# An encoder layer on one core: a fifth pair of weight row blocks by seven products, its low parts by an adding transfer

## The chip, the cores and the metric

The kernel runs on one core of a Trainium2 chip. The metric is the device time of one execution in microseconds (us), the median of several. The engines are named as in the profile: PE (TensorE matmul, PEld its weight load), DVE (VectorE), ACT (ScalarE), POOL (GpSimd), SP (SyncE, which issues most transfers). Each engine works through its own list of instructions in order and waits at an instruction until what it needs is there.

## The reference

One layer of a bidirectional encoder, 256 tokens of width 2048, all in float32:

```python
x = x + 0.5 * swiglu(rms_norm(x, ffn1_norm), ffn1_w_gu, ffn1_w_down)   # gate, up: 2048 -> 5632 each
proj = rms_norm(x, mix_norm) @ w_in            # query, key, value of two groups of heads
x = x + concat(group_A, group_B) @ w_out       # grouped-query and differential attention
x = x + 0.5 * swiglu(rms_norm(x, ffn2_norm), ffn2_w_gu, ffn2_w_down)
x = rms_norm(x, out_norm)

def swiglu(h, w_gu, w_down):
    g, u = split(h @ w_gu, 2)
    return (silu(g) * u) @ w_down
```

## The kernel before

Every float32 weight and activation is split in two parts, hi (a cast by ACT, L139) and lo (the weight minus hi, by DVE, L140), and every product is three matmuls: hi·hi, hi·lo, lo·hi. Weights come from HBM into `raw` (4 slots; two row blocks of 128 rows, j = 0 and 1, 1024 columns). ACT writes `whi`, DVE writes `wlo`; both have 4 slots, so two `raw` tiles are split ahead of PE, and slots are taken in turn: a row block takes the slot that the fourth row block before it had.

The two feed-forward parts (FFN) are the same code. The first 1024 gate columns and then the first 1024 up columns are done by `mm_block`. The other gate and up columns are done 512 at a time in `columns(i)`, i = 2 to 10; one call takes the 16 row blocks of the contraction in 8 pairs, for 512 gate columns (s = 0) and the same 512 up columns (s = 1). After each call but the last of an FFN comes one `down`, half of a group of the down projection (96 matmuls). So there are 18 calls of `columns` in all.

`PAIRS` says how a pair is done. False: 8 products (2 row blocks, 2 token halves, gate and up), 24 matmuls. True: 7 products after Strassen and Winograd, 21 matmuls. They need sums of weight blocks, which DVE forms in `Ta` and `Tb` (1024 columns each, L443, L445, L446) and which are split like weights (`Ta_hi`, `Ta_lo`, `Tb_hi`, `Tb_lo`, one slot each); of the second row block only the gate half is still split. The sums of x that the products need (`xs` for False, `xp` for True) are formed once in each FFN from `xT`, by functions put in the list `pending`, of which `pump()` runs one at set places.

`turn_block` brings 512 finished columns of gate times up into the layout of the next product: a transposition on DVE, 16 transfers of 32 KB on SP (`move`, L282), then two casts and two subtractions into `hT_hi` and `hT_lo`. `down` needs these.

The text of the program doesn't set the order on the engines: a scheduler sorts the instructions of each engine, before the run, by its own estimate of when each can start, and that order is then fixed. With c for the pair, the weights are split thus:

```python
n = 1 if pair and j == 1 else 2
splits.append(split(hi[:, :n], lo[:, :n], raw[:, j, :n]))
```

Of the kernel before, what the change touches and what calls it, by code (L numbers as in the profile page):

```python
# [20 lines left out]
P = 128  # L21
# [17 lines left out]
PAIRS = (False, True, False, True, False, True, False, True)  # L39
# [4 lines left out]
def encoder_layer(ctx: ExitStack, tc: tile.TileContext, a: dict, out: bass.AP):  # L44
# [96 lines left out]

    def new_rows():

        return (ht_p.tile([P, WB // P, T], F32R, name="hT_hi"), ht_p.tile([P, WB // P, T], F32R, name="hT_lo"))
# [31 lines left out]
    def mm_block(lhs, nk, w, row0, col0, width, evac, before=None, after=None, slots=1, t_major=None):  # L176
# [39 lines left out]
        if t_major is not None:  # L216
            with tc.manual_schedule(engines={mybir.EngineType.PE}):
                for c in range(nc_):
                    load(c)
                    for b in range(nb):  # L220
                        mm(b, 0, [2 * c, 2 * c + 1])
                        if c == nc_ - 1:
                            evac(b, 0, ps[b, 0])
                for b in range(nb):
                    step = 256 if b == nb - 1 else 512
                    for c0 in range(0, 512, step):
                        mm(b, 1, list(range(nk)), c0, c0 + step)
                        evac(b, 1, ps[b, 1], c0, c0 + step)
            return
        for c in range(nc_):  # L230
            if before is not None:
                before(c)
            load(c)
# [20 lines left out]
    def ffn(xT, norm, w_gu, w_down, half_done=None, before=None, after=None, last_evac=None, last_pools=None):  # L254
# [4 lines left out]
        with tc.tile_pool(name="ffn", bufs=1) as fp:  # L259
# [40 lines left out]
            sg = [fp.tile([P, WB], F32, name=f"sg{t}") for t in range(NT)]  # L300

            def evac_gate(b, t, ps):
                nc.scalar.activation(sg[t][:, b * 512:(b + 1) * 512], ps, AF.Silu, scale=norm.rstd[t][:, 0:1])

            if before is None:
                mm_block(rows(xT), NK, w_gu, 0, 0, WB, evac_gate)
            else:
                with tc.manual_schedule(engines={mybir.EngineType.SP}):
                    mm_block(rows(xT), NK, w_gu, 0, 0, WB, evac_gate, lambda c: before(c, ip), after)
            h0 = [fp.tile([P, NT, 512], F32, name="h", bufs=2) for b in range(2)]  # L310

            def evac_up(b, t, ps):
                nc.vector.scalar_tensor_tensor(h0[b][:, t, :], ps, norm.rstd[t][:, 0:1],
                                               sg[t][:, b * 512:(b + 1) * 512], op0=ALU.mult, op1=ALU.mult)


# [4 lines left out]
            rb = fp.tile([P, T], F32, name="rb")  # L321
# [26 lines left out]
            def paired_rows(c):  # L348
# [12 lines left out]
            pending.append(spread)  # L361
            pending.extend(functools.partial(paired_rows if pair else single_rows, c)
                           for c, pair in enumerate(PAIRS))
            ready = []
            pending.append(lambda: ready.append(True))
# [3 lines left out]
            for b in range(2):  # L369
                turn_block(b, h0[b])  # L370


            def columns(i):
# [9 lines left out]
                def mm(name, terms, end):  # L383
# [31 lines left out]
                for c, pair in enumerate(PAIRS):  # L415
# [5 lines left out]
                    for j in range(2):  # L421
# [3 lines left out]
                        splits.append(split(hi[:, :n], lo[:, :n], raw[:, j, :n]))  # L425
# [31 lines left out]
                    if c == last:  # L457
                        while pending:
# [5 lines left out]
                             ("p1", "p6", "p7", "c12", "c11", "c3", "c21"))  # L464
                    for m, name in enumerate(names):
                        mm(name, [product[name]], c == last)
                        if c == last:
                            done(name)
                        if m in (2, 6):
                            pump()  # L470
                turn_block(i, h)

            def down(j, half):
                c, width = j * WB, min(WB, DFF - j * WB)
                final = j == n_groups - 1
                while not set(range(2 * j, 2 * j + width // 512)) <= turned_blocks:
                    pump()
# [5 lines left out]
                mm_block(rows([hT[j]]), width // P, w_down, c, half * WB, WB, evac, slots=2, t_major=t_major)  # L483
# [16 lines left out]
    def load_xT(c, pool):  # L500

        raw = pool.tile([P, 2, 512], F32, name=("Ta", "Tb")[c % 2]).rearrange("p j f -> p (j f)")[:, :2 * T]
# [31 lines left out]
    with ExitStack() as mixer:  # L534
        mp = mixer.enter_context(tc.tile_pool(name="mix", bufs=1))
# [248 lines left out]
        def new_oT():  # L784
            return (mp.tile([P, WB // P, T], F32R, name="oT_hi", bufs=2),
                    mp.tile([P, WB // P, T], F32R, name="oT_lo", bufs=2))
# [117 lines left out]
```

## Time and profile before

| | |
|---|---|
| time, median of 3 | 1756.95 us (1756.93 to 1759.1) |
| the profiled execution, its own time | 1757.13 us |
| its span, first to last instruction | 1755.4 us |
| PE busy | 1731.7 us, 99% |
| DVE busy | 1400.5 us, 80% |
| ACT busy | 958.3 us, 55% |
| POOL busy | 48.2 us, 3% |
| bytes moved by the DMA engines | 355.81 MB |

The time of the profiled execution is 0.2 us over the median. Between its own time and its span lie 1.7 us at the two ends. A PE that reads as busy is not a PE at its peak, since matmuls overlap; what counts is how far apart they start.

### The profile page before, as it was taken

How to read it: one execution, taken by the hardware profiler on the slowest of the kernel's cores; microseconds unless marked ns; L12 is line 12 of the kernel's file. 1: busy time of each engine (PE TensorE's matmuls, PEld its weight loads, DVE VectorE, ACT ScalarE, POOL GpSimd, SP SyncE). 2: the span in 40 equal slices, each digit the busy share in tenths (PEclk: the TensorE clock that was granted, in tenths of full speed). 3: DMA queues.
4: the chain of work that ended last, by engine and by line, in shares of the span. 5: the costliest groups of instructions: out<-in, count | busy, mean ns of one | idle time of the engine just before them, and what ended most of it. 6: DMA issues, size and time to landing. Idle time of an engine off the chain costs nothing.

```text
span 1755.4 us, 21389 instructions
## 1 busy us (share of the span) xinstructions
PE 1731.7 (99%) x7652; PEld 1423.7 (81%) x7652; DVE 1400.5 (80%) x1729; ACT 958.3 (55%) x1359; POOL 48.2 (3%) x75
## 2 busy tenths in 40 slices
PE   9998999999999999999999999999999999999998
PEld 7876888888888888888788888867888888888886
DVE  6988989889889887646566565998889888988976
ACT  6555555555455554656776455555455455555544
POOL 0000000000000000122110000000000000000000
PEclk9999999999999999999999999999999999999999
DMA  9546665576566664655445455565566557656662
GB/s 368 189 161 216 212 237 193 176 248 210 183 245 204 203 209 162 219 189 196 156 173 195 145 199 184 173 232 189 202 214 220 185 201 242 205 186 240 220 227 98
DMA packets 165259, 355.81 MB, mean 203 GB/s; under 512 B 15600, under 2 KB 42656, under 8 KB 165024
## 3 DMA queue, kind: packets, MB, share of 16 engines
q1 hardware_dynamic: 164336, 353.10, 58.4%
q8 instruction: 60, 0.98, 0.2%
q10 hardware_dynamic: 720, 1.31, 0.2%
q14 instruction: 47, 0.39, 0.1%
q0 software_dynamic: 96, 0.02, 0.0%
HBM read 337.60 MB, written 2.10 MB: 194 GB/s over the span
## 4 chain that ended last, share of the span: by engine, by line
PE 90%; DMA 3%; DVE 2%; ACT 2%; SPq 2%; issue 1%; POOL 0%; POOLq 0%; ACTq 0%; DVEq 0%
PE psm L213 16%; PE psm L214 16%; PE psm L212 16%; PE psm L386 12%; PE psm L388 12%; PE psm L389 12%; DMA raw<-in_ffn_w_gu 1%; DMA raw<-in_w_in 1%; DVE wlo L140 1%; PE psx L386 1%; SPq L632 1%; PE psx L389 1%; PE psx L388 1%; DMA raw<-in_ffn_w_down 1%; SPq L282 1%
## 5 line engine op out<-in xcount | busy, mean ns | idle before, releaser
L140 DVE TENSOR_TENSOR wlo<-raw,whi 128x1024 fp32r<-128x1024 f32 (+1 forms) x644 | 713.7, 1140 | 208.3 <-ACT whi L139 204.2
L139 ACT CAST whi<-raw 128x1024 fp32r<-128x1024 f32 (+1 forms) x644 | 611.5, 984 | 480.3 <-PE psm L389 213.9
L213 PE MATMUL psm<-wlo,hT_hi 128*128 128x512 f32 x1252 | 487.8, 391 | 1.7 <-DVE wlo L140 1.7
L214 PE MATMUL psm<-whi,hT_lo 128*128 128x512 f32 x1252 | 486.3, 390 | 0.0
L212 PE MATMUL psm<-whi,hT_hi 128*128 128x512 f32 x1252 | 428.6, 391 | 4.8 <-ACT whi L139 2.1
L212 PEld LDWEIGHTS psm<-whi,hT_hi 128*128 128x128 f32 x1252 | 235.3, 188 | 56.2 <-ACT whi L139 2.9
L213 PEld LDWEIGHTS psm<-wlo,hT_hi 128*128 128x128 f32 x1252 | 235.8, 188 | 52.2 <-DVE wlo L140 3.6
L214 PEld LDWEIGHTS psm<-whi,hT_lo 128*128 128x128 f32 x1252 | 235.5, 188 | 48.2
L388 PE MATMUL psm<-wlo,xs 128*128 128x512 f32 x576 | 221.5, 390 | 0.7 <-DVE wlo L140 0.7
L389 PE MATMUL psm<-whi,xs 128*128 128x512 f32 x576 | 221.2, 389 | 0.0
L386 PE MATMUL psm<-whi,xs 128*128 128x512 f32 x576 | 196.6, 389 | 0.7 <-ACT whi L139 0.7
L388 PEld LDWEIGHTS psm<-wlo,xs 128*128 128x128 f32 x576 | 108.1, 188 | 24.2 <-DVE wlo L140 1.9
L386 PEld LDWEIGHTS psm<-whi,xs 128*128 128x128 f32 x576 | 108.0, 188 | 23.6 <-ACT whi L139 1.1
L389 PEld LDWEIGHTS psm<-whi,xs 128*128 128x128 f32 x576 | 108.1, 188 | 22.4
L139 ACT CAST Ta_hi<-Ta 128x1024 fp32r<-128x1024 f32 x72 | 75.6, 1051 | 91.0 <-DVE Ta L443 71.3
L443 DVE TENSOR_TENSOR Ta<-raw 128x1024 f32<-128x1024 f32 x72 | 87.9, 1220 | 39.2 <-DMA raw<-in_ffn_w_gu 39.0
L140 DVE TENSOR_TENSOR Tb_lo<-Tb,Tb_hi 128x1024 fp32r<-128x1024 f32 x72 | 87.8, 1219 | 2.7 <-ACT Tb_hi L139 0.8
L249 DVE SCALAR_TENSOR_TENSOR x<-psm,x 128x512 f32<-128x512 f32 (+1 forms) x113 | 73.1, 680 | 19.6 <-PE psm L214 19.4
L140 DVE TENSOR_TENSOR Ta_lo<-Ta,Ta_hi 128x1024 fp32r<-128x1024 f32 x72 | 87.7, 1219 | 0.2 <-ACT Ta_hi L139 0.2
L388 PE MATMUL psm<-wlo,xp 128*128 128x512 f32 x216 | 84.6, 392 | 0.0
L389 PE MATMUL psm<-whi,xp 128*128 128x512 f32 x216 | 84.5, 391 | 0.0
L386 PE MATMUL psm<-whi,xp 128*128 128x512 f32 x216 | 80.5, 390 | 0.4 <-ACT whi L139 0.4
(166 smaller groups left out, 1729.6 us busy)
## 6 DMA issues: line engine op xcount, KB each, us to landing
raw<-in_ffn_w_gu SPq DMA_DIRECT2D x288, 512.0 KB, 5.6
raw<-in_ffn_w_down SPq DMA_DIRECT2D x88, 1024.0 KB, 5.6
raw<-in_w_in SPq DMA_DIRECT2D x32, 1024.0 KB, 5.1
raw<-in_ffn_w_gu SPq DMA_DIRECT2D x30, 1024.0 KB, 5.9
raw<-in_w_out SPq DMA_DIRECT2D x16, 1024.0 KB, 5.0
h<-sg SPq DMA_DIRECT2D x352, 32.0 KB, 1.9
raw<-in_w_in SPq DMA_DIRECT2D x8, 512.0 KB, 3.6
heads<-near SPq DMA_DIRECT2D x96, 32.0 KB, 1.9
```

The costliest lines, as they stand in the source:

```text
L139: casts.append(nc.scalar.copy(hi, src))
L140: return nc.vector.tensor_tensor(lo, src, f32(hi), op=ALU.subtract)
L212: nc.tensor.matmul(o, xh, wh, start=k == 0, stop=False)
L213: nc.tensor.matmul(o, xh, wl, start=False, stop=False)
L214: nc.tensor.matmul(o, xl, wh, start=False, stop=k == nk - 1)
L249: nc.vector.scalar_tensor_tensor(x[t][:, s], ps[:, c0:c1], scale, x[t][:, s], op0=ALU.mult, op1=ALU.add)
L282: nc.sync.dma_start(turned[q * B32:(q + 1) * B32, :, i_, :], near[0][i_ * B32:(i_ + 1) * B32, :, q, :])
L386: nc.tensor.matmul(bank[name], xh, wh, start=name not in begun, stop=False)
L388: nc.tensor.matmul(bank[name], xh, wl, start=False, stop=False)
L389: nc.tensor.matmul(bank[name], xl, wh, start=False, stop=end and m == n - 1)
L443: nc.vector.tensor_tensor(ta, flat[:, 3:4, :].broadcast_to([P, 2, 512]), flat[:, 1:3, :], op=ALU.subtract)
L632: nc.sync.dma_start(far[q * B32:(q + 1) * B32, i], near[i * B32:(i + 1) * B32, q].rearrange("p h d -> p (h d)"))
```

## The change

It has four parts. (1) `PAIRS[0]` becomes True: 5 of 8 pairs by 7 products. (2) For the True pairs 0, 1, 3 and 5 of each call, the lo part of row block j = 0 is no longer a subtraction on DVE. ACT writes minus hi into `wlo`, and then a transfer issued by POOL adds `raw` to it (512 KB, in place). The two matmuls that read this lo part (hi·lo of the products c11 and c3) are written down last in the pair. (3) The sums of x are put in `pending` sooner: after chunk 6 of the first `mm_block` of FFN 1, before the first one of FFN 2. (4) Block 1 of `turn_block` follows block 0 after six idle places, and `down` waits for the block that its chunk reads and not for both. Beside these: `xT` is loaded into three other tiles, `rb` lies in `junk`, and `oT_hi` and `oT_lo` get a pool of their own.

```diff
-PAIRS = (False, True, False, True, False, True, False, True)
+PAIRS = (True, True, False, True, False, True, False, True)
...
+    def split_by_transfer(hi, lo, src):
+        casts.append(nc.scalar.copy(hi, src))
+        nc.scalar.activation(lo, f32(hi), AF.Copy, scale=-1.0)
+        nc.gpsimd.dma_start(f32(lo), src, accum_op=ALU.add)
...
         for c in range(nc_):
             if before is not None:
                 before(c)
+            if need is not None:
+                need(c)
             load(c)
...
+            def after_load(c):
+                after(c)
+                if c == 6:
+                    form_sums()
...
+            if before is None:
+                form_sums()
...
-            for b in range(2):
-                turn_block(b, h0[b])
+            turn_block(0, h0[0])
+            pending.extend([idle] * 6)
+            turn_block(1, h0[1])
...
-                        nc.tensor.matmul(bank[name], xh, wl, start=False, stop=False)
+                        if later is None:
+                            nc.tensor.matmul(bank[name], xh, wl, start=False, stop=False)
+                        else:
+                            later.append((bank[name], xh, wl))
...
-                        splits.append(split(hi[:, :n], lo[:, :n], raw[:, j, :n]))
+                        if pair and j == 0 and c < last:
+                            split_by_transfer(*(part.rearrange("p s f -> p (s f)") for part in (hi, lo, raw[:, j])))
+                        else:
+                            splits.append(split(hi[:, :n], lo[:, :n], raw[:, j, :n]))
...
+                    for o, xh, wl in later:
+                        nc.tensor.matmul(o, xh, wl, start=False, stop=False)
...
-                while not set(range(2 * j, 2 * j + width // 512)) <= turned_blocks:
-                    pump()
+                def need(c):
+                    while 2 * j + c // 2 not in turned_blocks:
+                        pump()
```

How the instructions stand now, at two places. The number behind a tile is that of its buffer, L404, L407, L410 and L497 are matmuls of a pair in the changed program, L219 and L220 matmuls of `down`.

**Start of a call of columns, ACT.** These are rows of ACT where `columns(9)` of FFN 1 begins, before the change: pair 0 is the two casts from `raw_4501`, pair 1 those from `raw_4536`.

```order
L139 CAST whi_4459<-raw_4453 128x1024
L139 CAST Tb_hi_4556<-Tb_4548 128x1024
L139 CAST whi_4504<-raw_4501 128x1024
L139 CAST whi_4508<-raw_4501 128x1024
L139 CAST hT_hi_4449<-h_3989 128x8x2x32 x2
L139 CAST whi_4539<-raw_4536 128x1024
L139 CAST whi_4543<-raw_4536 128x512
L139 CAST Ta_hi_4632<-Ta_4627 128x1024
```

And the same place in the changed program: pair 0 is `raw_4601`, pair 1 `raw_4647`; `whi_4559` is the last row block of the `down` before.

```order
L139 CAST whi_4559<-raw_4553 128x1024
L144 CAST whi_4604<-raw_4601 128x1024
L145 ACTIVATE wlo_4605<-whi_4604 128x1024
L139 CAST whi_4609<-raw_4601 128x512
L144 CAST whi_4650<-raw_4647 128x1024
L139 CAST whi_4655<-raw_4647 128x512
L145 ACTIVATE wlo_4651<-whi_4650 128x1024
L139 CAST hT_hi_4549<-h_4075 128x8x2x32 x2
L139 CAST Ta_hi_4664<-Ta_4659 128x1024
```

The write of minus hi for pair 1 (`wlo_4651`) now stands behind the cast into `whi_4655`, and the casts of `hT_hi` and `Ta_hi_4664` behind it. `whi_4655` takes the slot of `whi_4559`, four row blocks before.

**Start of a call of columns, PE.** First the end of `down` in PE's list of the changed program, with the last matmul that reads `whi_4559`:

```order
L219 MATMUL psm_4458<-wlo_4560,hT_hi_3501 128x512
L220 MATMUL psm_4458<-whi_4559,hT_lo_3502 128x512
L497 MATMUL psm_4594<-wlo_4605,xp0_129 128x512
L497 MATMUL psm_4595<-wlo_4605,xp0_129 128x512
L404 MATMUL psm_4594<-whi_4650,xp0_129 128x512
L410 MATMUL psm_4594<-whi_4650,xp1_130 128x512
```

From the row behind that L220 on, 21 matmuls stand ahead of the first that reads `wlo_4651`, the tile that the transfer of pair 1 completes:

```order
L407 MATMUL psm_4597<-wlo_4656,xp0_129 128x512
L410 MATMUL psm_4597<-whi_4655,xp1_130 128x512
L404 MATMUL psm_4596<-Tb_hi_4622,xp0_129 128x512
L407 MATMUL psm_4596<-Tb_lo_4623,xp0_129 128x512
L410 MATMUL psm_4596<-Tb_hi_4622,xp1_130 128x512
L497 MATMUL psm_4594<-wlo_4651,xp0_129 128x512
L497 MATMUL psm_4595<-wlo_4651,xp0_129 128x512
L404 MATMUL psx_4599<-Ta_hi_4664,xp0_129 128x512
L404 MATMUL psm_4593<-Ta_hi_4664,xp0_129 128x512
L407 MATMUL psx_4599<-Ta_lo_4665,xp0_129 128x512
```

The scheduler has moved the two L497 of pair 1 ahead of that pair's products with `Ta` and `Tb` (`Ta_hi_4664` and on), so in PE's list they are not last.

**End of the first call, columns(2), ACT.** Before the change, with `h_497` for block 1 of `turn_block`:

```order
L139 CAST Ta_hi_1121<-Ta_1116 128x1024
L139 CAST whi_1206<-raw_1203 128x1024
L139 CAST whi_1210<-raw_1203 128x512
L139 CAST Tb_hi_1125<-Tb_1117 128x1024
L139 CAST hT_hi_1016<-h_497 128x8x2x32 x2
L139 CAST Ta_hi_1219<-Ta_1214 128x1024
```

In the changed program, where block 1 is `h_541` and `whi_1282` to `whi_1327` belong to the `down` that follows:

```order
L139 CAST Ta_hi_1214<-Ta_1209 128x1024
L139 CAST Tb_hi_1218<-Tb_1210 128x1024
L139 CAST whi_1282<-raw_1280 128x1024
L139 CAST whi_1286<-raw_1280 128x1024
L139 CAST whi_1323<-raw_1321 128x1024
L139 CAST whi_1327<-raw_1321 128x1024
L139 CAST hT_hi_1030<-h_541 128x8x2x32 x2
L417 COPY sg0_1245<-psm_880 128x512
```

The casts of block 1 stood ahead of the sums of the last pair (`Ta_hi_1219`); they now stand behind all pairs of the call, and what is behind them is the copy of the first product (L417).

## Rows read from the trace of the kernel before

**Rows 1.** The page, part 1: busy us (share of the span) xinstructions.

```profile
PE 1731.7 (99%) x7652; PEld 1423.7 (81%) x7652; DVE 1400.5 (80%) x1729; ACT 958.3 (55%) x1359; POOL 48.2 (3%) x75
```

**Rows 2.** Windows of three column periods: busy us per engine (xinstructions), clock, DMA share, GB/s.

```profile
342.50:405.07 62.57, 62.57 (x278) 51.83 (x277) 55.27 (x62) 33.00 (x39) 0.00 (x0) 1.00 0.62 210
405.07:467.63 62.56, 62.56 (x277) 51.82 (x277) 55.14 (x62) 32.99 (x39) 0.00 (x0) 1.00 0.62 210
467.63:530.19 62.56, 62.56 (x277) 51.82 (x277) 54.49 (x62) 32.87 (x38) 0.00 (x0) 1.00 0.62 211
```

**Rows 3.** Windows of the two starts of columns, PE alone: busy (xinstructions), clock, DMA, GB/s.

```profile
120.00:160.00 40.00, 34.59 (x138) 0.96 0.58 207
1140.00:1200.00 60.00, 54.51 (x222) 0.97 0.54 180
```

**Rows 4.** Timeline of ACT there: start, us, what, [idle before <- releaser].

```profile
134.19 1.14 ACT L139 CAST hT_hi<-h 128x512 fp32r<-128x512 f32 x2 [7.25 <-DMA h<-sg]
135.24 1.04 ACT L139 CAST Ta_hi<-Ta 128x1024 fp32r<-128x1024 f32 x1
```

**Rows 5.** Groups by form, one period (405.07 to 467.63): count, busy us, mean ns.

```profile
L140 DVE TENSOR_TENSOR wlo<-raw,whi 128x1024 fp32r<-128x1024 f32 x21 | 24.9, 1219 | 5.2 <-ACT whi L139 5.1
L139 ACT CAST whi<-raw 128x1024 fp32r<-128x1024 f32 x21 | 21.4, 1048 | 17.1 <-PE psm L389 12.0 <-PE psm L214 5.1
L443 DVE TENSOR_TENSOR Ta<-raw 128x1024 f32<-128x1024 f32 x4 | 4.9, 1221 | 1.8 <-DMA raw<-in_ffn_w_gu 1.8
L445 DVE TENSOR_TENSOR Tb<-raw,Ta 128x512 f32<-128x512 f32 x4 | 2.8, 692 | 0.1
L140 DVE TENSOR_TENSOR wlo<-raw,whi 128x512 fp32r<-128x512 f32 x4 | 2.7, 684 | 0.0
```

**Rows 6.** Timeline at the start of one call, PE and then ACT.

```profile
416.69 0.39 PE L214 MATMUL psm<-whi,hT_lo 128*128 128x512 f32 x1
416.92 0.39 PE L388 MATMUL psm<-wlo,xs 128*128 128x512 f32 x1
...
417.12 0.62 ACT L139 CAST whi<-raw 128x512 fp32r<-128x512 f32 x1 [1.07 <-PE psm L214]
```

**Rows 7.** Transfers of 32 KB within SBUF (L282), the same period.

```profile
DMA to landing us min/median/max: 1.8/1.9/3.4
```

**Rows 8.** The fastest stretch of transfers: window of 1 us, PE alone.

```profile
136.00:137.00 1.00, 0.67 (x2) 1.00 1.04 430
```

**Rows 9.** Weight loads of 512 KB in columns (L420), the same period.

```profile
L420 SPq DMA_DIRECT2D raw<-in_ffn_w_gu x16: 540/596/815, 412.6 to 459.5; - x16
...
DMA to landing us min/median/max: 3.6/5.4/8.3
```

**Rows 10.** Transfers issued by POOL (L80, 8 KB): issue ns min/median/max, then landing.

```profile
L80 POOL DMA_DIRECT2D gain_ffn_norm<-in_ffn_norm x2: 537/636/736, 1.3 to 2.6; - x2
...
DMA to landing us min/median/max: 4.3/5.2/5.2
```

**Rows 11.** Windows at the start of the call of rows 5 and later in it.

```profile
415.00:420.00 5.00, 5.00 (x24) 4.14 (x23) 5.00 (x8) 1.67 (x3) 0.00 (x0) 1.00 0.99 319
420.00:425.00 5.00, 5.00 (x24) 4.14 (x23) 3.12 (x5) 1.84 (x2) 0.00 (x0) 1.00 1.03 379
...
438.00:443.00 5.00, 5.00 (x24) 4.14 (x23) 4.79 (x6) 1.81 (x2) 0.00 (x0) 1.00 0.90 349
```

**Rows 12.** Timeline of PE: the longer waits.

```profile
136.33 0.50 PE L386 MATMUL psx<-Ta_hi,xp 128*128 128x512 f32 x1 [3.10 <-ACT Ta_hi L139]
840.36 1.64 PE L212 MATMUL psm<-whi,hT_hi 128*128 128x512 f32 x4 [1.81 <-ACT whi L139]
1168.18 0.91 PE L386 MATMUL psm<-Tb_hi,xp 128*128 128x512 f32 x2 [1.81 <-ACT Tb_hi L139]
1193.23 0.50 PE L213 MATMUL psm<-wlo,hT_hi 128*128 128x512 f32 x1 [1.01 <-DVE wlo L140]
```

**Rows 13.** Windows behind the first three of them, PE alone: busy (xinstructions), granted clock.

```profile
138.00:141.00 3.00, 3.00 (x8) 0.50 1.03 388
1169.00:1172.00 3.00, 2.96 (x8) 0.50 1.01 410
841.00:844.00 3.00, 3.00 (x9) 0.50 0.07 14
```

More of the change, by code (lines that the diff above doesn't have):

```diff
@@ L174, in late_load, with mm_block @@
             nc.sync.dma_start(dst, src)
-    def mm_block(lhs, nk, w, row0, col0, width, evac, before=None, after=None, slots=1, t_major=None):
+    def mm_block(lhs, nk, w, row0, col0, width, evac, before=None, after=None, slots=1, t_major=None, need=None):
         nb = width // 512
@@ L232, in mm_block @@
                 before(c)
+            if need is not None:
+                need(c)
             load(c)
@@ L297, in turn_block @@
                 pending.append(lambda: turned_blocks.add(i))
[L300 to L314, printed above, removed]
             single = [k for c, pair in enumerate(PAIRS) if not pair for k in (2 * c, 2 * c + 1)]
@@ L359, in paired_rows, with evac_gate, form_sums, evac_up @@
                 split(xp[0][:, i, 3:7, :], xp[1][:, i, 3:7, :], z)
-            pending.append(spread)
-            pending.extend(functools.partial(paired_rows if pair else single_rows, c)
-                           for c, pair in enumerate(PAIRS))
-            ready = []
-            pending.append(lambda: ready.append(True))
+            sg = [fp.tile([P, WB], F32, name=f"sg{t}") for t in range(NT)]
+            def evac_gate(b, t, ps):
+                nc.scalar.activation(sg[t][:, b * 512:(b + 1) * 512], ps, AF.Silu, scale=norm.rstd[t][:, 0:1])
+            def form_sums():
+                pending.append(spread)
+                pending.extend(functools.partial(paired_rows if pair else single_rows, c)
+                               for c, pair in enumerate(PAIRS))
+                pending.append(lambda: ready.append(True))
+            def after_load(c):
+                after(c)
+                if c == 6:
+                    form_sums()
+            ready = []
+            if before is None:
+                form_sums()
+                mm_block(rows(xT), NK, w_gu, 0, 0, WB, evac_gate)
+            else:
+                with tc.manual_schedule(engines={mybir.EngineType.SP}):
+                    mm_block(rows(xT), NK, w_gu, 0, 0, WB, evac_gate, lambda c: before(c, ip), after_load, slots=2)
+            h0 = [fp.tile([P, NT, 512], F32, name="h", bufs=2) for b in range(2)]
+            def evac_up(b, t, ps):
+                nc.vector.scalar_tensor_tensor(h0[b][:, t, :], ps, norm.rstd[t][:, 0:1],
+                                               sg[t][:, b * 512:(b + 1) * 512], op0=ALU.mult, op1=ALU.mult)
             mm_block(rows(xT), NK, w_gu, 0, DFF, WB, evac_up, slots=2)
@@ L381, in columns, with mm @@
                 last = len(PAIRS) - 1
-                def mm(name, terms, end):
+                def mm(name, terms, end, later=None):
                     n = len(terms)
@@ L464, in columns @@
                              ("p1", "p6", "p7", "c12", "c11", "c3", "c21"))
+                    later = []
                     for m, name in enumerate(names):
-                        mm(name, [product[name]], c == last)
+                        mm(name, [product[name]], c == last, later if name in ("c11", "c3") and c < last else None)
                         if c == last:
@@ L482, in down @@
                 evac = last_evac(half) if final and last_evac else add_to_x(half, 0.5)
-                mm_block(rows([hT[j]]), width // P, w_down, c, half * WB, WB, evac, slots=2, t_major=t_major)
+                mm_block(rows([hT[j]]), width // P, w_down, c, half * WB, WB, evac, slots=2, t_major=t_major, need=need)
                 if final and half_done:
@@ L500, in load_xT @@
     def load_xT(c, pool):
-        raw = pool.tile([P, 2, 512], F32, name=("Ta", "Tb")[c % 2]).rearrange("p j f -> p (j f)")[:, :2 * T]
+        raw = f32(pool.tile([P, 2, 512], F32R, name=("Ta_hi", "Tb_hi", "Ta_lo")[c % 3]).rearrange("p j f -> p (j f)")[:, :2 * T])
         raw = raw.rearrange("p (j t) -> p j t", j=2)
@@ L534, in encoder_layer @@
     with ExitStack() as mixer:
+        ot_p = mixer.enter_context(tc.tile_pool(name="ot", bufs=2))
         mp = mixer.enter_context(tc.tile_pool(name="mix", bufs=1))
```

6 lines of the change are left out of this document (3 added, 3 removed).

## The prediction

> **What bounds the kernel now.** I began with the busy shares: PE 99%, DVE 80%, ACT 55% [rows 1]. Then windows along the span, to see whether PE is full everywhere. In the 18 calls of columns it is: one call and the `down` behind it take 62.56 us, PE has no idle time in them, and DVE is busy 55 of 62.6 us and ACT 33 [rows 2]. The program has 96 + 4 x 24 + 4 x 21 = 276 matmuls there, so one starts every 62.56 / 276 = 0.2267 us (the rows also count those that reach over an edge). What takes matmuls out of this stretch is paid in full, and so is every wait put in front of PE. The two places where PE does wait are the first calls of the FFNs: 5.4 us of 40 and 5.5 us of 60 [rows 3]. The timeline of ACT shows why: it waited 7.25 us for the small transfers of `turn_block` at the casts of block 1, with `Ta_hi`, which PE needed, queued behind [rows 4].
>
> **Seven products in a fifth pair.** 3 matmuls less in each of 18 calls are 54 x 0.2267 = 12.2 us.
>
> **DVE and ACT.** For each call DVE loses four subtractions of 1.22 us (4.9) and gains, for pair 0, `Ta`, `Ta_lo` and `Tb_lo` (1.22 each), two half-width sums (0.69 each) and a subtraction of half the width (0.68 for 1.22): 4.5 us [rows 5]. That is 0.4 us less of 55, with 7 us free. ACT gains four writes of minus hi and two casts of full width, less half a cast: about 6 us on 33. I cost both at nothing; they are hidden by PE, which is full. Without that cover ACT's part would be up to 6 us a call.
>
> **The transfer and what waits for it.** This is the term that decides. 72 transfers of 512 KB are issued by POOL, in whose list only the next transfer stands behind them. PE's order says what they may take. Take pair 1 in the steady calls. ACT's write of minus hi stands behind the cast into `whi_4655`, and this cast needs the slot that the last L220 of `down` reads. Before, the same cast stood at the same place: it started 0.20 us after the next matmul did and took 0.62 us [rows 6]. Minus hi is as wide as a full cast, 1.05 us [rows 5], so POOL can start 0.20 + 0.62 + 1.05 = 1.87 us after that matmul. PE reaches `wlo_4651` 21 matmuls later, at 4.76 us. So the transfer has **2.9 us** from its issue to its landing before PE stands still, and everything behind in PE's list with it. Counted in the same way, pair 0 has 8.39 - 0.20 - 2 x 1.05 = 6.1 us (37 matmuls), pair 3 about 11 us, pair 5 6.35 - 0.20 - 1.05 = 5.1 us (28 matmuls). This order stands in 10 of the 18 calls. In the other eight the scheduler has laid it otherwise; the tight places there have 2.9 and 4.0 us in columns(2) of FFN 1 and FFN 2, 5.6 and 4.2 in columns(3), 3.8 for pair 5 in columns(4) and 4.6 for pair 1 in columns(5).
>
> How long does the transfer take? No row shows one that adds. From below: 32 KB within SBUF land in 1.8 us at best [rows 7], and the other 480 KB at the fastest rate seen, 430 GB/s [rows 8], take 1.14: 2.94 us. That would be a plain copy with the engines free, issued by SP. Three rows speak for more. A weight load of 512 KB lands in 3.6 us at best, 5.4 in the median and 8.3 at most [rows 9]. POOL's own loads of only 8 KB took 4.3 to 5.2 us, their issue alone 0.54 to 0.74, though at the cold start [rows 10]. And at the start of a call the loads already fill the engines, at a share of 0.99 to 1.03, and 0.90 later where pair 5 falls [rows 11]; the transfer would share them. Adding also has to read the destination: 512 KB more, 1.2 us at 430 GB/s. I take **5.4 us**: the row nearest in size, engines and place. Both ends, 2.94 and 8.3, go into the range.
>
> The Trainium skill speaks against the change here: by its page "Collectives: The Full Stack" (section "The bandwidth ceiling: the fold count and why AG ≠ RS ≠ AR") an add in the transfer engines needs two source reads on one ring, and that halves its rate against a copy. No row here shows an add. With the fixed part and rate of the page named under the first rival, 1 MB read would be 4.4 us, an estimate, and the sum by it about the time before.
>
> With 5.4 us the wait is 2.5 us for pair 1 and 0.3 for pair 5: 2.8 us in each of 10 calls, 28 us. In the other eight it is 2.5 + 1.4 + 1.2 + 2 x 1.6 + 2 x 0.8 = 9.9 us. What is late next: all of PE; DVE and ACT gain slack by it.
>
> **The clock.** PE waited 1.81 us or more three times after the start, and each time about 3 us at a granted clock of 0.50, the 1.2 GHz level, followed [rows 12, 13]; after 1.01 us it did not fall. In 3 us at that level 8 matmuls started where 13.2 fit: 5.2 x 0.2267 = 1.2 us lost, about 1.4 with the edges. A wait of 2.5 us is on the far side of this, so each of the 10 calls, and one of the others, pays 1.4 more: 15.4 us.
>
> **Sums sooner, blocks apart.** In the first call of each FFN, ACT's casts of block 1 no longer stand ahead of a sum that PE needs; they stand behind all pairs of the call. At most this gives back both places' idle time, 10.9 us, and 1.6 us of slow clock each: 14 us. At least nothing, since these 16 small transfers may hold up the copy behind them (L417), and with it `down`, instead. I take half, 7 us.
>
> The edits of `load_xT`, `rb`, `ot_p` and `need` cost nothing: no engine does more for them, and PE's first chunks are bound by the weights.
>
> **Sum.** 1757.1 (the profiled execution; the median is 0.2 less) - 12.2 - 7 + 28 + 9.9 + 15.4 = **1791 us**, 1.9% slower. A tenth of a microsecond in the transfer is 1 to 2 us in the time.
>
> **Rivals.**
> *The transfer is a fast copy (faster than before).* With the engines free to it and the add costless, it lands in 2.94 to 4.1 us. For it: the lower bound above, and loads that did land in 3.6. Against it: the median of 5.4 in the same stretch. At 3.6 us the 10 calls wait 0.7 each and one of the others 0.7, under the 1.0 us that left the clock alone: 1757.1 - 19.2 + 7.7 = 1746 us; at 2.94, 1738 us. The sign turns at about 4.4 us. The page "DMA: Bandwidth & Descriptors" of the Trainium skill (section "Anatomy of one DMA — SWDGE (gpsimd) path") gives a transfer issued by POOL 2.0 us and its bytes at 436 GB/s, for 512 KB 3.2 us. By that this rival would win, at about 1741 us, an estimate. The loads of [rows 9] don't bear it out where the engines are full.
>
> *Gain and wait cancel.* At 4.4 us: 10 x 1.5 + 3.3 = 18 us of waits against 19 us: 1756 us. It would be 1770 if 1.5 us of waiting already brings the slow clock; the rows leave that open between 1.01 and 1.81.
>
> *The transfer is slower still, and pair 5 waits too.* At 6.5 us (adding, and half the engines' time): 10 x (3.6 + 1.4) + 21.7 in the others + 17 x 1.4 for the clock = 95.5 us, so 1833 us; at 8.3, beyond 1880.
>
> *Late weights.* A `raw` slot is free only when its transfer has landed; pair 5's load waits for pair 1's. It would be issued 1.9 + 5.4 = 7.3 us after that first matmul and land 5.4 later, at 12.7. Its cast needs a slot that PE frees 63 matmuls on, at 14.3 us, and PE's wait of 2.5 pushes that to 16.8. A longer transfer moves both alike, so this costs nothing unless loads take 4 us more than their median; then 18 us for each further one.
>
> **How the numbers follow.** Forecast (transfer between 4.7 and 6 us): chance 0.42, 1765 to 1815. Slower still: 0.20. Cancel (4.1 to 4.7): 0.11. Fast copy: 0.27. A measurement of this kernel can tell about 0.2%, 3.5 us, from no change. So faster 0.27, same 0.10, slower 0.63. The range reaches from inside the fast copy (3.2 us) to a transfer of some 6.7 us: 1740 to 1845.
>
> **What would show it.** Right: a group of PE waits for `wlo<-raw` at L497, some 2.5 us once a call, with POOL as issuer; a median from issue to landing near 5.4 us; a granted clock near 0.9 in windows at the start of calls; 90 sums `Ta` on DVE in place of 72; no wait for `Ta_hi` in the first calls. Wrong: calls of 61.9 us with PE full, or landings under 4 us. It would fail if the adding transfer runs ahead of queued loads, or if the add in the engines is many times slower than a copy.

## The result and the profile after

The changed kernel takes **1855.5 us** (median of four, 1851.9 to 1859.6) against 1757.9 us for the kernel before (median of four; the table in front has three of them): 1.0553 times the time before, interval 1.0532 to 1.0574. It is slower, as forecast, but by 98 us where 34 were forecast, and 10 us beyond the range.

Part 1 of the page of the changed kernel (span 1857.8 us), which answers to [rows 1]:

```profile
PE 1758.9 (95%) x7598; PEld 1425.1 (77%) x7598; DVE 1392.6 (75%) x1753; ACT 1056.4 (57%) x1467; POOL 110.5 (6%) x147
```

PE does 54 matmuls less, 12.2 us of work, and is yet busy 27.2 us longer. So its matmuls take 39.4 us more than they would at the old pace, and the time in which PE does nothing rose from 1755.4 - 1731.7 = 23.7 us to 98.9, by 75.2. The sum, 39.4 + 75.2 - 12.2 = 102.4, is the difference of the two spans. Of the 39.4 us, some 25 are the lower clock (what the granted level took from PE's busy time, summed over the two traces: 29.6 us against 5.1). The rest was not taken apart; some of it arises at the waits, where the matmul ahead of a wait counts with its whole 0.39 us and not with the 0.23 us to the next start. Windows of two steady calls, which answer to [rows 2] (busy us of PE, PEld, DVE, ACT, POOL, then clock, DMA share, GB/s), and of the microseconds behind the wait at 1611.13, PE alone:

```profile
1543.11:1611.13 68.02, 64.95 (x274) 51.99 (x274) 54.61 (x63) 38.69 (x44) 3.47 (x4) 0.97 0.74 227
1611.13:1679.28 68.15, 64.98 (x274) 51.99 (x274) 54.41 (x63) 38.53 (x44) 3.44 (x4) 0.97 0.72 221
...
1612.00:1614.00 2.00, 1.61 (x5) 0.69 1.03 384
1614.00:1616.00 2.00, 2.00 (x6) 0.50 1.05 400
1616.00:1618.00 2.00, 2.00 (x10) 0.96 1.04 390
```

A call takes 68 us where 273 matmuls of 0.2267 us would be 61.9: 68.02 - 64.95 = 3.1 us of waiting, and 3.1 us by which PE is busy longer. Of the latter the 1.2 GHz level takes, by the three short windows, 2 x (0.31 + 0.50 + 0.04) = 1.7 us in the second of the calls. What PE waited for (us in total, times, longest), in the whole program:

```profile
PE psx L404 <- ACT Ta_hi L139: 25.0, 15, 2.2
PE psm L218 <- ACT sg L417: 21.7, 2, 11.0
PE psm L497 <- DMA wlo<-raw: 13.7, 17, 3.3
PE psm L219 <- DVE wlo L140: 9.6, 15, 2.6
```

The wait that the prediction was about, L497 for the transfer, is there, 17 times, but it is the third: 13.7 us. The first is for `Ta_hi`, a cast of ACT. The line view of the transfers (issue ns min/median/max, then the landing) shows them slower in the median than the 5.4 us taken:

```profile
L146 POOL DMA_DIRECT2D wlo<-raw x72: 852/862/948, 90.9 to 1762.7; - x72
...
DMA to landing us min/median/max: 4.6/6.3/10.3
```

The median mixes places, though. In the call of the next fence the transfers of pairs 0 and 1 landed in 5.0 us each, those of pairs 3 and 5 in 8.1 and 9.6.

Why `Ta_hi` was late is read backwards in the timeline of one call (start, us, what, [idle before <- releaser]): PE, ACT, SP, then DVE. The last matmul of `down` starts at 1603.10.

```profile
1608.68 0.73 PE L497 MATMUL psm<-wlo,xp 128*128 128x512 f32 x2 [0.44 <-DMA wlo<-raw]
1611.13 0.50 PE L404 MATMUL psx<-Ta_hi,xp 128*128 128x512 f32 x1 [1.71 <-ACT Ta_hi L139]
...
1608.99 1.14 ACT L139 CAST hT_hi<-h 128x512 fp32r<-128x512 f32 x2 [5.65 <-DMA h<-sg]
1610.04 1.04 ACT L139 CAST Ta_hi<-Ta 128x1024 fp32r<-128x1024 f32 x1
...
1593.50 11.17 SPq L291 DMA_DIRECT2D h<-sg  x16
1604.77 12.19 SPq L441 DMA_DIRECT2D raw<-in_ffn_w_gu  x10
...
1584.03 1.21 DVE L467 TENSOR_TENSOR Ta<-raw 128x1024 f32<-128x1024 f32 x1
...
1586.36 0.68 DVE L469 TENSOR_TENSOR Tb<-raw,Ta 128x512 f32<-128x512 f32 x1
1586.96 0.68 DVE L430 TENSOR_TENSOR h<-sg,sg 128x512 f32<-128x512 f32 x1
1587.56 1.22 DVE L140 TENSOR_TENSOR Ta_lo<-Ta,Ta_hi 128x1024 fp32r<-128x1024 f32 x1
1588.70 0.68 DVE L470 TENSOR_TENSOR Tb<-raw,Tb 128x512 f32<-128x512 f32 x1
1589.30 0.68 DVE L434 TENSOR_TENSOR h<-sg,sg 128x512 f32<-128x512 f32 x1
1589.90 1.22 DVE L467 TENSOR_TENSOR Ta<-raw 128x1024 f32<-128x1024 f32 x1
1591.04 1.22 DVE L140 TENSOR_TENSOR wlo<-raw,whi 128x1024 fp32r<-128x1024 f32 x1
1592.17 1.30 DVE L285 STREAM_TRANSPOSE sg<-h 128x512 f32<-128x512 f32 x2
```

The same place in the kernel before, DVE, SP and then ACT (there `down` ends with the matmul of 416.69 in [rows 6]):

```profile
398.60 0.68 DVE L409 TENSOR_TENSOR h<-sg,sg 128x512 f32<-128x512 f32 x1
399.39 0.69 DVE L413 TENSOR_TENSOR h<-sg,sg 128x512 f32<-128x512 f32 x1
400.11 1.30 DVE L276 STREAM_TRANSPOSE sg<-h 128x512 f32<-128x512 f32 x2
...
401.44 11.01 SPq L282 DMA_DIRECT2D h<-sg  x16
412.56 18.33 SPq L420 DMA_DIRECT2D raw<-in_ffn_w_gu  x12
...
413.95 1.14 ACT L139 CAST hT_hi<-h 128x512 fp32r<-128x512 f32 x2 [1.68 <-DMA h<-sg]
```

Pair 0's sums (`Ta` at 1584.03, `Tb` at 1586.36 and 1588.70, `Ta_lo` at 1587.56), which are new, stand on DVE among the steps that finish `h` and ahead of its transposes; the next `Ta`, pair 1's, at 1589.90 now does so as well. So the transposes start 10.9 us ahead of that last matmul; before, 16.6 us. SP moves the block 5.7 us later, and the weight loads of the call, behind the moves on the same queue, start 1.7 us after the last matmul of `down`; before, 4.1 us ahead of it. The moves also land later: `hT_hi` starts 4.3 us after the last one is issued (1604.67), 1.5 us before. `Ta_hi` of pair 1 stands behind `hT_hi`, as the order in front showed, and PE behind `Ta_hi`.

The two waits of 11 us stand in the first calls. ACT there, and PE:

```profile
148.43 1.14 ACT L139 CAST hT_hi<-h 128x512 fp32r<-128x512 f32 x2 [9.11 <-DMA h<-sg]
149.47 0.58 ACT L417 COPY sg<-psm 128x512 f32<-128x512 f32 x1
...
150.10 0.80 PE L218 MATMUL psm<-whi,hT_hi 128*128 128x512 f32 x1 [11.05 <-ACT sg L417]
```

The casts of block 1 hold up the copy L417, which frees the bank that `down` needs: the order that the prediction named as its worse end, where it booked nothing instead of a loss.

### The profile page after: what moved, and what is told of

It is laid out like the page before. It is cut to its first block, busy times and chain, and to the rows that moved or that the text cites. A ratio compares the mean times of both kernels' runs of the same rounds, so it can differ in the third digit from the quotient of the medians.

```text
span 1857.8 us, 21733 instructions
## 1 busy us (share of the span) xinstructions
PE 1758.9 (95%) x7598; PEld 1425.1 (77%) x7598; DVE 1392.6 (75%) x1753; ACT 1056.4 (57%) x1467; POOL 110.5 (6%) x147
## 3 DMA queue, kind: packets, MB, share of 16 engines
q0 software_dynamic: 10464, 37.78, 10.9%
## 5 line engine op out<-in xcount | busy, mean ns | idle before, releaser
L140 DVE TENSOR_TENSOR wlo<-raw,whi 128x1024 fp32r<-128x1024 f32 (+1 forms) x572 | 627.2, 1113 | 203.5 <-ACT whi L139 183.5
L139 ACT CAST whi<-raw 128x1024 fp32r<-128x1024 f32 (+1 forms) x572 | 534.1, 961 | 324.4 <-PE psm L410 143.9
L219 PE MATMUL psm<-wlo,hT_hi 128*128 128x512 f32 x1252 | 490.7, 394 | 9.7 <-DVE wlo L140 9.6
L220 PE MATMUL psm<-whi,hT_lo 128*128 128x512 f32 x1252 | 487.6, 392 | 0.0
L219 PEld LDWEIGHTS psm<-wlo,hT_hi 128*128 128x128 f32 x1252 | 236.5, 189 | 65.0 <-DVE wlo L140 16.6
L220 PEld LDWEIGHTS psm<-whi,hT_lo 128*128 128x128 f32 x1252 | 236.5, 189 | 48.2
L407 PE MATMUL psm<-wlo,xs 128*128 128x512 f32 x432 | 169.8, 394 | 0.4 <-DVE wlo L140 0.4
L410 PE MATMUL psm<-whi,xs 128*128 128x512 f32 x432 | 169.4, 393 | 0.0
L404 PE MATMUL psm<-whi,xs 128*128 128x512 f32 x432 | 160.3, 402 | 0.0
L146 POOL DMA_DIRECT2D wlo<-raw x72 | 62.3, 866 | 1241.6 <-ACT wlo L145 874.8
L139 ACT CAST Tb_hi<-Tb 128x1024 fp32r<-128x1024 f32 x90 | 94.4, 1048 | 60.3 <-DVE Tb L470 54.8
L144 ACT CAST whi<-raw 128x1024 fp32r<-128x1024 f32 x72 | 75.5, 1048 | 92.2 <-PE psm L220 77.6
L140 DVE TENSOR_TENSOR Ta_lo<-Ta,Ta_hi 128x1024 fp32r<-128x1024 f32 x90 | 109.8, 1220 | 9.4 <-ACT Ta_hi L139 8.1
L404 PE MATMUL psm<-whi,xp 128*128 128x512 f32 x270 | 106.0, 393 | 6.9 <-ACT whi L139 6.6
L410 PE MATMUL psm<-whi,xp 128*128 128x512 f32 x270 | 105.2, 389 | 0.0
L404 PEld LDWEIGHTS psm<-whi,xs 128*128 128x128 f32 x432 | 84.9, 197 | 19.7 <-ACT whi L139 0.8
```

The costliest lines, as they stand in the source:

```text
L139: casts.append(nc.scalar.copy(hi, src))
L140: return nc.vector.tensor_tensor(lo, src, f32(hi), op=ALU.subtract)
L144: casts.append(nc.scalar.copy(hi, src))
L146: nc.gpsimd.dma_start(f32(lo), src, accum_op=ALU.add)
L219: nc.tensor.matmul(o, xh, wl, start=False, stop=False)
L220: nc.tensor.matmul(o, xl, wh, start=False, stop=k == nk - 1)
```

## Experiments

Two theories went in. **Turn:** the block's transposes are late on DVE, and everything behind them with it. **Landing:** the transfers themselves are slow or in the way.

### One part at a time

`no_transfer` is the changed kernel (the two matmuls of each pair stay last) with

```diff
-                        if pair and j == 0 and c < last:
-                            split_by_transfer(...)
-                        else:
-                            splits.append(split(hi[:, :n], lo[:, :n], raw[:, j, :n]))
+                        splits.append(split(hi[:, :n], lo[:, :n], raw[:, j, :n]))
```

> The changed kernel with all low parts subtracted on DVE again, no transfer; five pairs, the sooner sums and the blocks apart stay. Theory 'turn' (the transposes of a block stand about 4 us later on DVE because the sums of pair 0 now stand ahead of them, and its small transfers land about 3 us later because they share the transfer engines with the adding transfers; ACT does its list in order, so Ta_hi of pair 1 stands behind the late casts of hT_hi): the small transfers land in 1.9 us again, the casts of hT_hi come about 3 us sooner, and PE's waits of 1.7 to 2.2 us for Ta_hi are gone or under 0.5; only the two waits of 11 us for the copy L417 in the first calls stay: 1757 - 12 + about 25 = 1770 us (1760 to 1785). Rival 'landing' (PE's loss comes from the transfers themselves): all waits vanish with them, and the first calls too: 1738 to 1750 us. Rival 'fifth pair' (pair 0's sums alone do it, whoever moves the bytes): Ta_hi waits stay, 1820 us or more.

1779.7 us (1.0121, 1.0097 to 1.0144; here and below the time over that of the kernel before, and its interval): within the range of "turn", and out of that of both rivals. PE's waits for `Ta_hi` fell from 25.0 to 4.7 us; 18.5 us for L417 are left.

`old_order` is the kernel before with `PAIRS = (True, ...`, `rb` in the junk tile, `split_by_transfer` and the list `later`, nothing else.

> The kernel before with the fifth pair and the adding transfers alone: the sums of x, the two blocks of the first call and the wait of down for both its blocks are as before. Theory 'turn': the 18 calls lose as in the changed kernel (68 us a call), the two waits of 11 us for L417 go and the old ones of 3.1 and 1.8 us come back: about 1855 - 27 + 7 = 1835 us. Rival (sooner sums and blocks apart give back about 7 us, as the prediction took): about 1862 us.

1848.3 us (1.052, 1.0496 to 1.0545): between the two expectations.

`four_pairs` is the changed kernel with

```diff
-PAIRS = (True, True, False, True, False, True, False, True)
+PAIRS = (False, True, False, True, False, True, False, True)
```

> The changed kernel with pair 0 done in four products again: transfers for pairs 1, 3 and 5 only (54). Theory 'turn': without pair 0's sums the transposes stand about 4 us sooner and no transfer shares the engines with the block's small transfers but that of pair 1; PE's wait for Ta_hi is gone, calls of 62.6 plus about 1 us, and the two waits of 11 us stay: 1757 + 25 + 18 = 1800 us. Rival 'landing': pair 1 keeps its short time from issue to use, so its waits stay and PE does 12 us more work: 1855 us or more.

1827.5 us (1.0387, 1.0362 to 1.0412): between the two expectations. Without pair 0's sums the waits for `Ta_hi` fell to 3.4 us, as "turn" says, but PE now waits 21.6 us for low parts from DVE.

`fifth_only` is the kernel before with `PAIRS` as changed and `rb = junk.bitcast(F32)`.

> The kernel before with the fifth pair alone (rb in the junk tile, for room): no transfer, sums of x and blocks in the old order. Theory 'turn': pair 0's sums push the transposes 4 us back, but with all low parts on DVE the small transfers land in 1.9 us and the time in hand before (about 3 us at the casts of hT_hi) nearly covers it: 1757.8 - 12.2 + 0 to 10 = 1750 us (1745 to 1757). Rival 'fifth pair' (the sums in that place cost by themselves): 1770 us or more.

1776.4 us (1.0093, 1.0076 to 1.011). The rival wins: the fifth pair with 54 matmuls less costs 18 us by itself. (DVE also has more to do here than in the changed kernel, 83% of the span for 75%, since it subtracts all low parts again.) Its timeline of ACT at one call's start shows the late turn without any transfer, and the weights behind it:

```profile
1601.55 1.15 ACT L139 CAST hT_hi<-h 128x512 fp32r<-128x512 f32 x2 [2.64 <-DMA h<-sg]
1602.60 1.05 ACT L139 CAST Ta_hi<-Ta 128x1024 fp32r<-128x1024 f32 x1
1604.63 1.05 ACT L139 CAST whi<-raw 128x1024 fp32r<-128x1024 f32 x1 [0.97 <-DMA raw<-in_ffn_w_gu]
```

`transfer_only` is `old_order` with four pairs and `rb` in its own tile.

> The kernel before with the transfers alone: four pairs, 54 transfers (pairs 1, 3 and 5 of each call), sums of x and blocks in the old order. If the transfers cost by their own landing and what they hold back, about 3 us a call: 1810 us (1800 to 1820). If they cost only together with the late turn of the fifth pair: 1757 to 1770 us.

1810.0 us (1.029, 1.0268 to 1.0311). So against before: fifth pair +18, transfers +51, both together +91, and the first calls' new order about 7 on top, at the edge of what the two intervals tell. Neither of the two gains. The two together lose some 22 us more than they do apart, but that is no sign that one makes the other dearer: `old_order` has 72 transfers and `transfer_only` 54, and the 18 of pair 0 cost some 25 us by themselves in `skip_pair0` below. In `transfer_only` it is the weights that are late: DVE's `Ta` waited 185.2 us for loads of `raw`, before the change 39.0.

### Is it the turn?

`casts_late` puts the casts of `hT` behind `Ta_hi` and `Tb_hi` of pair 1 on ACT:

```diff
-... for i0 in (0, 2)] + [idle])
+... for i0 in (0, 2)] + [idle] * 7)
-                    with tc.issue_after(splits[-1].ins):
+                    with tc.issue_after(splits[-1].ins), tc.issue_after(casts[-1].ins):
                         split(hi, lo, src)
```

> The changed kernel with six idle steps more ahead of the casts of hT, and these casts behind the last cast issued by then on ACT, so that Ta_hi and Tb_hi of pair 1 stand ahead of them; nothing else moves. Theory 'turn': the waits for Ta_hi and Ta_lo (30.7 us) and the slow clock behind them go, calls fall from 68 to about 63 us: 1855 - 70 = 1785 us (1770 to 1800), with the two waits of 11 us left. Rival 'landing': PE then waits for the transfer of pair 1 by as much, within 10 us of 1855.

1858.0 us (1.0569, 1.0538 to 1.06): no gain, the number of the rival, though the wait that took over is in the main another than it named. The waits for `Ta_hi` fell to 9.4 us and others took their place. PE's waits:

```profile
PE psm L404 <- ACT whi L139: 31.3, 14, 3.6
...
PE psm L497 <- DMA wlo<-raw: 20.6, 14, 4.8
```

The timeline of ACT and SP at one call's start:

```profile
1680.13 1.04 ACT L139 CAST whi<-raw 128x1024 fp32r<-128x1024 f32 x1 [2.58 <-DMA raw<-in_ffn_w_gu]
...
1662.70 12.50 SPq L291 DMA_DIRECT2D h<-sg  x16
1675.30 19.93 SPq L441 DMA_DIRECT2D raw<-in_ffn_w_gu  x12
```

The late casts were only the last link. The weight loads behind the moves are as late, and they were next. So the delay has to be undone at its root, the transposes. `turn_first` does that to the changed kernel:

```diff
+                    with tc.issue_after(turns[-1].ins) if c == 0 and turns else ExitStack():
                         nc.vector.tensor_tensor(ta, ...)
                         nc.vector.tensor_tensor(tb[:, 0], ...)
                         nc.vector.tensor_tensor(tb[:, 1], ...)
```

where `turns` collects the transposes. (The edit moves the lines behind it down by one: L497 is L498 here.)

> The changed kernel with one order pinned on DVE: the sums Ta and Tb of pair 0 are issued behind the transposes of the block before (in the changed kernel they stand among the sums of its products and ahead of its transposes). Theory 'turn': the transposes, the small transfers behind them on SP and the weight loads behind those all start 4 to 5 us sooner against the call; waits for Ta_hi go, and calls fall from 68 to 63 or 64 us: 1785 us (1770 to 1805), the two waits of 11 us still in it. Rival 'landing' (transfers of 6 to 7 us hold raw slots and share the engines, so something else is late in the same place): 1835 us or more.

1819.2 us (1.0345, 1.0327 to 1.0362): 36 us better, half of what the theory gave. The timeline of DVE and SP, at a call whose `down` ends with the matmul of 1505.59:

```profile
1488.60 1.30 DVE L285 STREAM_TRANSPOSE sg<-h 128x512 f32<-128x512 f32 x2
...
1489.93 10.28 SPq L291 DMA_DIRECT2D h<-sg  x16
1500.32 17.81 SPq L441 DMA_DIRECT2D raw<-in_ffn_w_gu  x10
```

PE's waits, and from the line view the transfers' landing:

```profile
PE psx L404 <- ACT Ta_hi L139: 17.7, 15, 2.1
PE psm L498 <- DMA wlo<-raw: 13.0, 15, 3.5
```

```profile
DMA to landing us min/median/max: 4.6/8.0/10.4
```

The transposes start 17.0 us ahead of that matmul and the loads 5.3 us, as before the change (16.6 and 4.1), and `hT_hi` does not wait in this call. But the transfers now meet the loads and land in 8.0 us in the median. So the late turn is a part of the steady loss, and what is left was looked for in the transfers.

### What in the transfers?

`plain_copy` takes the add away, `nc.gpsimd.dma_start(f32(lo), src)` without `accum_op`.

> The changed kernel with the 72 transfers as plain copies: nothing is added, so the low part of these row blocks holds the weights themselves and not what the high part leaves of them. If the add is what makes the transfer slow (it reads the destination too), its landing falls from 6.3 us to 5 or less and the time by 30 us or more, to 1825 us or less. If the landing is set by the engines that it shares with weight loads and block moves, it stays near 6 us and the time within 12 us of 1855.

1810.2 us (1.0299, 1.0271 to 1.0327): 45 us less, as the first expectation has it, in the landing too. Issue and landing:

```profile
L146 POOL DMA_DIRECT2D wlo<-raw x72: 530/530/635, 91.0 to 1721.2; - x72
...
DMA to landing us min/median/max: 2.9/5.0/9.4
```

The add costs 0.33 us at the issue and, from issue to landing, 1.7 us at best and 1.3 in the median; 512 KB more at the 430 GB/s of [rows 8] would be 1.2.

`late_pairs` is `turn_first` with transfers for pairs 3 and 5 alone (`c in (3, 5)` for `c < last`, here and for `later`).

> The kernel of turn_first (1819 us) with transfers for pairs 3 and 5 only; pairs 0 and 1 are split on DVE. If it is the transfers at a call's start that cost, where weight loads, block moves and transfers share the engines, calls come down to about 62.5 us: 1785 us, nearly all above 1757 - 12 being the two waits of 11 us and a few more in the first calls. If each transfer costs alike, by the raw slot it holds: half of what is left of it, 1800 us or more.

1774.2 us (1.0091, 1.0076 to 1.0106), 45 us less than `turn_first` and better than both expectations. The window of one call, from one block move to the next:

```profile
1399.32:1461.42 62.10, 62.10 (x275) 51.16 (x274) 56.53 (x65) 36.70 (x41) 1.71 (x2) 1.00 0.72 231
```

A call of 62 us with PE full, though DVE is busier (56.5 us) than in the changed kernel, and though these transfers land in 9.0 us in the median. The loss left is in the first calls: 23.2 us for L417.

`skip_pair0` and `skip_pair1` are `turn_first` with `c in (1, 3, 5)` and `c in (0, 3, 5)`.

> The kernel of turn_first (1819 us) without the transfer of pair 0, which is split on DVE: transfers for pairs 1, 3 and 5. If PE's short time in hand at pair 1 (2.9 us by the prediction, 6.1 for pair 0) is what the transfers cost: about 1819 us still. If transfers at the call's start cost by sharing the engines and the raw slots: half of the 45 us to late_pairs goes, 1797 us.

> The kernel of turn_first without the transfer of pair 1: transfers for pairs 0, 3 and 5. If it is PE's short time in hand at pair 1: all of the 45 us go, 1774 us. If sharing and slots: 1797 us.

1793.7 (1.0202) and 1796.1 us (1.0215): each takes away about half of the 45, as the second expectation has it. But the two runs don't test the short time in hand at pair 1, since `turn_first` no longer has it: the order on PE is another there, and in the call of the fence above the transfer of pair 1 was issued at 1506.93 and first needed at 1516.15, 9.2 us later. What they show is that the transfer of pair 0 costs some 25 us there and that of pair 1 some 23, though PE's waits for transfers (13.0 us in `turn_first`, 13.8 and 14.5 without one of them) hardly change. Both stand in the stretch where the engines are full and hold a `raw` slot there. SP shows the slots in the changed kernel (us in total, times, longest), a wait that the kernel before cannot have:

```profile
SPq L199 <- DMA wlo<-raw: 143.8, 22, 10.8
...
SPq L441 <- DMA wlo<-raw: 35.0, 8, 8.4
```

These sums are no measure of a loss. Before the change SP waited 829.5 us for the subtractions on DVE that held the same slots, and in `late_pairs`, whose steady calls lose next to nothing, it waited 288.3 us for transfers. That the engines are shared shows in the weight loads: the 32 of two calls landed in 7.3 us in the median in `turn_first` (1426 to 1554) and in 4.8 in `late_pairs` (1461 to 1586). How the 45 us divide between full engines and slots held was not told apart.

### The first calls, and what is worth having

`blocks_together` is the changed kernel without `pending.extend([idle] * 6)`.

> The changed kernel without the six idle steps between the two blocks of each first call. Theory (the casts of block 1 stand ahead of the copy L417 only since these steps put them at the call's end): both waits of 11 us for L417 go, with 2 to 3 us of slow clock each: 1830 us (1825 to 1838). Rival (the casts then stand ahead of the sums of a pair, as in the kernel before, and the waits for Ta_hi there take the place): 1845 to 1855 us.

1841.4 us (1.0475, 1.0458 to 1.0493): 14 us better, between the two. The waits of 11 us are gone (0.8 us is left for this copy); waits for transfers, 24.5 us in place of 13.7, took part of it back. So against `old_order` (1848.3 us) the new order of the first calls loses 7 us with the idle steps and gains 7 us without them.

`fifth_turn_first` is `fifth_only` with the pin of `turn_first`.

> The kernel before with the fifth pair, and the sums of pair 0 issued behind the transposes of the block before; no transfer, sums of x and blocks in the old order. If the place of these sums on DVE is what made the fifth pair alone cost 18 us, the calls come down to 62 to 62.5 us and the gain of 54 matmuls shows: 1750 us (1745 to 1757), faster than both kernels. Rival (DVE at 83% and loads behind the block moves hold the calls back whatever the order): 1765 us or more.

1761.0 us (1.0013, 1.0004 to 1.0021): between the two expectations. The pin is worth 15 us here, but the 12 us of the matmuls don't show in the time. PE still waits 12.0 us for `Ta_hi`, most of it in FFN 1. A call of FFN 2 and one of FFN 1:

```profile
1447.46:1509.27 61.81, 61.81 (x274) 51.19 (x273) 58.49 (x67) 34.27 (x39) 0.00 (x0) 1.00 0.64 213
...
470.86:535.74 64.88, 62.22 (x275) 51.08 (x274) 58.73 (x67) 34.44 (x40) 0.00 (x0) 1.00 0.60 203
```

In FFN 2 most calls run with PE all but full, though DVE is busy 58.5 of 61.8 us; there DVE's load alone, the ground of the rival, doesn't hold them back. Why the calls of FFN 1 lose up to 3 us each was not pursued.

`late_pairs_old_order` is `fifth_turn_first` with transfers for pairs 3 and 5.

> The kernel before with the fifth pair, transfers for pairs 3 and 5 alone, the sums of pair 0 behind the transposes, and the first calls' sums of x and blocks in the old order. If the calls then run at 61.9 us with PE full and only the old waits of the first calls are left: 1774 - 30 = 1745 us (1740 to 1752), faster than both kernels. If the sooner sums and the blocks apart were not what cost about 30 us in the first calls: 1760 us or more.

1773.5 us (1.0083, 1.0066 to 1.0101), a miss: in place of L417, PE waited 20.3 us for transfers, most of it in the first two calls of each FFN (2.4, 4.6, 5.1 and 3.8 us). With transfers in them, the first calls lose 20 us in either order.

`late_pairs_late_calls` adds `and i > 3` to that, and `pair5_late_calls` is the same for `c == 5` alone.

> The kernel of fifth_turn_first (1761 us: fifth pair, sums of pair 0 behind the transposes, old order of the first calls) with transfers for pairs 3 and 5 in the calls from columns(4) on alone (28 transfers in 14 calls). If the transfers take the load off DVE where they have time, the later calls run at 61.9 us, and the waits for transfers of 2.4 to 5.1 us in the first two calls of each FFN, which late_pairs_old_order showed, are gone: 1748 us (1744 to 1754), faster than both kernels. If the later calls don't gain by it: 1760 us or more.

> The same with the transfer of pair 5 alone (14 transfers). One transfer a call holds fewer raw slots, but takes only half as much off DVE: if one is enough for calls of 61.9 us, 1748 us as well; if DVE still holds the casts back, between 1750 and 1760 us.

1760.5 us (1.0015, 1.0005 to 1.0024) and 1774.6 us (1.0087, 1.0075 to 1.01): the first at the number of its second expectation, though most of its later calls do run at about 62 us, the second beyond both. Leaving the first calls out is worth 13 us, as the waits there said. But no kernel of these beats the one before. The page of `late_pairs_late_calls` (its profiled execution, 1756.3 us, was the shortest of eleven):

```profile
PE 1724.9 (98%) x7598; PEld 1413.5 (81%) x7598; DVE 1438.6 (82%) x1797; ACT 1014.2 (58%) x1423; POOL 73.8 (4%) x103
```

Full matmuls would be 1731.7 - 12.2 = 1719.5 us; 5.4 us more of busy PE and 6 us more of doing nothing (1754.6 - 1724.9 = 29.7 against 23.7) eat the gain. Why one transfer a call is worse than none or two was not pursued.

## Why the prediction was off

**The direction and what bounds the kernel** were right: PE, with every wait put in front of it paid in full, and the transfer a loss and not a gain. The 12.2 us of the matmuls are real (calls of 62 us in `late_pairs`).

**The step that failed first is "DVE and ACT: I cost both at nothing".** The amounts held: 54.6 us of DVE a call, less than before. But what is added stands at another place than what is taken away. Pair 0's sums fall between the last products and the block's transposes, where DVE is the head of a chain: transposes, moves on SP, loads behind them, casts on ACT, PE. Pinning the sums behind the transposes gave back 36 of the 98 us in the changed kernel. Without transfers the fifth pair cost 18 us in place of a gain of 12, and the pin gave back 15 of these 30; the other 15, most of them in FFN 1, stay open.

In sum: without the 54 matmuls the kernel before would take 1757.9 - 12.2 = 1745.7 us, 110 less than the changed kernel. Taken away in this order, the place of the sums is worth 36 of them and the transfers of pairs 0 and 1 are worth 45; of the 28 left in `late_pairs`, 23 are the waits for L417.

**The transfer.** The landing was taken at 5.4 us. It is 6.3 in the median, but for pair 1, where it counted, it was about right: 5.0 us in the call shown. The lower bound, 2.94 us for a plain copy, was met by 2.9. What failed is the time in hand at pair 1, taken at 2.9 us on the ground that the cast into `whi_4655` waits for the last matmul of `down`. In the call shown that matmul starts at 1603.10, and this cast and the issue stand thus:

```profile
1601.75 0.62 ACT L139 CAST whi<-raw 128x512 fp32r<-128x512 f32 x1
...
1603.63 0.86 POOL L146 DMA_DIRECT2D wlo<-raw  x1 [5.20 <-PE psm L220]
```

The cast starts 1.35 us ahead of that matmul; POOL issues at 1603.63 and PE arrives at 1608.24, so that 4.6 us were in hand. So the direct wait was over-sized, 13.7 us for 37.9, and the cost stood elsewhere. "Late weights", a rival costed at nothing, is the closest to it: in `turn_first` the transfers of pairs 0 and 1 cost 45 us, half each, where PE had time for them and the weight loads beside them landed later.

The Trainium skill's page "Collectives: The Full Stack" (section "The bandwidth ceiling: the fold count and why AG ≠ RS ≠ AR") says of a ring's ReduceScatter that its add needs two source reads and so runs at half the rate of a copy; it does not speak of a transfer on one core. The trace agrees as far as it goes: 1.7 us more at best than the copy, where another 512 KB read would be 1.2. The fit of the Trainium skill's page "DMA: Bandwidth & Descriptors" (section "Anatomy of one DMA — SWDGE (gpsimd) path") gives 3.2 us for 512 KB, an estimate. That is near the best copy, 2.9, and well under its median, 5.0: the measurement decides.

**The clock** had the right mechanism and too few cases: 15.4 us forecast, some 25 measured. The prediction left open what lies between waits of 1.01 and 1.81 us; here the level of 0.50 followed a wait of 1.71 with 0.53 behind it.

**Sums sooner, blocks apart** was booked as a gain of 7 us with a worse end of nothing. The six idle steps cost 14 us; the rest of the new order gained about 7. The text named the copy L417 and then bounded its price at zero; 11 us twice was what the trace gave.

Of the rivals, "slower still" with 6.5 us for the transfer was nearest, at 1833 us, but by luck: the waits at L497 that it adds up were not there, and it lacked the turn and the late loads.

## What to carry to other kernels

When work is swapped on an engine that has slack, compare the places, not the totals: look at what stands behind the new instructions in that engine's list, and follow it over the queues to the engine that bounds. A wait that is removed at its last link (`casts_late`) comes back at the next; undo it at the head of the chain. And a transfer that takes work off an engine also holds its source buffer until it lands: place it where the transfer engines and the buffers have room.

## What the runs showed of the hardware

- An adding transfer of 512 KB within SBUF, issued by POOL, held POOL for 0.86 us (a plain one 0.53) and landed in 4.6 us at best and 6.3 in the median (2.9 and 5.0).
- Its landing changes with its place: in one call of the changed kernel 5.0 us for pairs 0 and 1, 8.1 and 9.6 for pairs 3 and 5. The median is 8.0 in `turn_first` and 9.0 in `late_pairs`, where PE waited only 6.4 us for transfers in all.
- Weight loads of 512 KB landed in 7.3 us in the median where such transfers ran beside them (two calls of `turn_first`), and in 4.8 where the transfers of pairs 0 and 1 were left out (two calls of `late_pairs`).
- PE's granted clock went to 0.50, the 1.2 GHz level, for some 3 us behind waits of 1.71 and 0.53 us in a row.
